# Down projection's held tiles prepared among earlier columns, mLSTM output transposes behind a step's gate products, forget gates a row chunk on, in a hybrid decoder layer

## The chip, the cores and the metric

One core of a Trainium2 chip runs the whole layer in one launch. The metric is the device time of one execution in microseconds; a kernel's time is the median of its runs. Matrix products run on TensorE (PE in the profile; its weight loads are PEld), elementwise work on VectorE (DVE) and ScalarE (ACT), and all loads are issued by SyncE's queue (SPq). Sums of products are kept in eight PSUM banks of 128 x 512 floats.

## The reference

One decoder layer on 256 tokens with a model width of 2048, all in float32:

```python
h = layer_norm(x) * (1.0 + sc1) + sh1
y = token_mixer(h, ...)                  # one input projection for everything below
x = layer_norm(ALPHA * x + g1 * y, ln_g[l, 0], ln_b[l, 0])
h = layer_norm(x) * (1.0 + sc2) + sh2
y = conv_ffn(h, w_up, conv_w, conv_b, w_down)
x = layer_norm(ALPHA * x + g2 * y, ln_g[l, 1], ln_b[l, 1])
...
# token_mixer: attention with gates (y_nsa) and mLSTM (y_ml), merged by gates
merged = sigmoid(merge_nsa) * (y_nsa @ w_br_nsa) + sigmoid(merge_ml) * (y_ml @ w_br_ml)
y = merged @ w_o
...
# mlstm, at its end: h normalised per head, times norm_g, times sigmoid(o)
# conv_ffn: (silu(causal_dwconv(a)) * g) @ w_down, with a and g of 5632 columns each
```

The shifts, scales and gates (sh, sc, g) come from a second input vector through a 2048 x 12288 product.

## The kernel before

Every weight is streamed once from memory in tiles of 512 KB. To keep float32 accuracy on TensorE, each weight tile w is split into a rounded part wh (ScalarE's cast, L154) and a remainder wl (VectorE's subtraction, L160), and each product is three matmuls: wh with the high and with the low part of the activations, and wl with the high part. `load_split` (L148 on) does load, cast and subtraction for one tile. There are seven w buffers, four wh and four wl (`WB`, L42). A load waits until a w buffer is free, a cast until a wh buffer is free, which is when TensorE has used the tile four places earlier.

The order of instructions on an engine is fixed when the program is built, and each engine takes its own in order: an instruction that waits holds up everything behind it on that engine. In places (`tc.manual_schedule`) the order is the order of the code for the engines named there; elsewhere a scheduler orders the instructions by what it reckons to be ready. Beside the main line, VectorE works off the conditioning product by multiply-accumulates on weight tiles (L279), spread over the whole kernel.

**Input projection.** Its last group of row chunks works through columns c = 0 to 5 with k the row chunk (loop at `for c in range(6)`, near L860). `steps` is a generator of the small gate computations of the mLSTM; `next(steps)` inside that loop (L873) moves it on by one step in the columns c = 3 and 4. Its product of the forget gates' cumulative sum is the PSUM tile ps_F, which waits for VectorE's subtraction at L706.

**Attention output and mLSTM output.** `nsa_out(g, t, ...)` gives the attention output of one group and one half of the rows in five steps for t = 1; in each step a block of probabilities is transposed on TensorE (ps_pT, L1044), ScalarE casts it (pT, L951), VectorE takes the remainder (vq or vx, L1055), and the products of earlier blocks are added into ps_y. `outs` (L1142) puts one tile of the merge gates' product (`fill(1)`, tile ps_mg, 12 matmuls) behind every step. In the last call, `outs(1, 1, ml_outs())`, the mLSTM output transposes `ml_out(h)` (L1119 on; four transposes into ps_yT, then y_mlT by ScalarE at L1128 and VectorE at L1129) are taken on by `next(beside, None)` ahead of the step's fill. ps_pT, ps_yT and ps_y share a pool of four PSUM banks, and ps_y keeps one. Branch products (ps_br with y_mlT and later with y_nsaT) are the next stage; the merge gates that are still in banks (ps_mg) must be emptied by two sigmoids (gt) before the branch product of y_nsaT can take their banks, and the gates kept in memory (gates0) are put through eight sigmoids (at L1203).

**Down projection, second half** (`proj_rows`, L1271 on, called with `hold`). The rows of the weight are 22 chunks of 128. The first 1536 output columns are three passes of 512 columns, each with 11 tiles (33 tiles), 12 matmuls a tile, for both halves of the rows (ps_d0, ps_d1). The last 512 columns are two half columns of 256, of six tiles each. The second of these uses held tiles: a tile is loaded, multiplied by the gate g2 on VectorE (L1306), cast on ScalarE into a kept buffer (L181) and given its remainder on VectorE (L182). They are held because the products of row half 1 come last, after all of row half 0. In the kernel before they are made inside the two half-column loops, and the scheduler spreads them over the end. After each pass VectorE adds the sum to the residual row (zt L1256, xz L1261) and takes statistics (L1265); the last residuals, the final layer norm and its stores follow (L1656 on).

Of the kernel before, what the change touches and what calls it, by code (L numbers as in the profile page):

```python
# [14 lines left out]
P = 128  # L15
# [15 lines left out]
NDOWN = 4 * 11  # L31
# [49 lines left out]
def build(ctx: ExitStack, tc: tile.TileContext, d, out, dbg=None):  # L81
    nc = tc.nc
# [44 lines left out]
    def load(src, after=None):  # L127
        n = src.shape[-1]
        t = wp.tile([P, 1024], F32, name="w", tag="w", bufs=WB[0])
        ins = nc.sync.dma_start(t[:, :n], src)  # L130
        if after:
            behind(ins, after)
        loaded[:] = [ins]
        return t
# [45 lines left out]
    def split_into(t, hi, lo):  # L180
        nc.scalar.copy(hi, t)  # L181
        nc.vector.tensor_sub(lo, t, hi)  # L182
# [260 lines left out]
    ready = [FIRST]  # L443
# [349 lines left out]
    for gi, kn in enumerate(GROUPS):  # L793
# [66 lines left out]
        for c in range(6):  # L860
            pss = [bank(psm, "ps_a%d" % t) for t in range(2)]
            aw = AW if c < 4 else 512
            for k in range(k0, k0 + kn):
                need(k)
                wh, wl = next(wa if c < 4 else wv)
                if k or c:
                    for t in range(2):
                        mm_a(pss[t][:, :aw], hT, k, t, wh, wl, k == k0, k == k0 + kn - 1)
                else:
                    for x, w in ((0, wh), (1, wh), (0, wl)):  # L870
                        for t in range(2):
                            mm(pss[t][:, :aw], hT[:, k, x, t * P:(t + 1) * P], turns(w), not x and w is wh, False)
                if not nxt and c in (3, 4) and (k - k0) % 3 == 2:  # L873
                    next(steps)
            for t in range(2):
                src = pss[t][:, :aw]
                if c < 4:
                    dst = projA[:, t, c * AW:(c + 1) * AW]
                else:
                    dst = mv1[:, t, 2 * c - 8:2 * c - 6, :MDV]  # L880
                    src = src.rearrange("p (h v) -> p h v", v=MDV)
                if gi == 0:
                    moved.append(lambda dst=dst, src=src: nc.scalar.copy(dst, src))
                else:
                    nc.vector.tensor_add(dst, src, dst)
            if not nxt:
                if c == 2:
                    while comp:
                        work()
                    Pk = pa.tile([P, 16, 48], F32R, name="Pk", tag="c4")  # L890
                    nTr = pa.tile([36, 384], F32R, name="nTr", tag="xe")
                    steps = gate_steps(Pk, nTr)
                    next(steps)
# [43 lines left out]
    def fill(n, rate=RATES[0]):  # L937

        for _ in range(n):
            if next(filler, 1) is None:  # L940
                tk.tick(rate)
# [177 lines left out]
    def ml_out(h):  # L1119
        ps = bank(psa, "ps_yT")  # L1120
        for c in range(2):
            for t in range(2):
                nc.tensor.transpose(ps[:, (2 * c + t) * P:(2 * c + t + 1) * P],
                                    num[:, h, t, c * P:(c + 1) * P], ident)
        for c in range(2):
            ng = prm[:, R_NG + 2 * h + c:R_NG + 2 * h + c + 1]
            src, hi = ps[:, c * S:(c + 1) * S], y_mlT[:, 2 * h + c, 0, :]
            nc.scalar.activation(hi, src, AF.Copy, scale=ng)  # L1128
            nc.vector.scalar_tensor_tensor(y_mlT[:, 2 * h + c, 1, :], src, ng, hi,  # L1129
                                           op0=ALU.mult, op1=ALU.subtract)  # L1130

    def ml_outs():
        for h in range(MH):
            yield
            ml_out(h)

    Ws, Pts = [], {}

    def probs(g, t):
        Pts[g, t] = nsa_probs(g, t)  # L1140

    def outs(g, t, beside=iter(())):  # L1142
        for _ in nsa_out(g, t, Pts.pop((g, t))):
            next(beside, None)
            fill(1)

    with tc.manual_schedule(engines={mybir.EngineType.PE}):
        fill(2, GR2)
        for _ in steps:
            pass  # L1150
        fill(2, GR2)
        for h in range(MH):
            Ws.append(ml_weights(h))
            fill(1)
        probs(0, 0)
        fill(2)
        num = pa.tile([P, MH, 2, MDV], F32, name="num", tag="m8")
        for h in range(MH):
            ml_num(h, Ws[h])
            if h % 2:  # L1160
                fill(h // 2 + 1)
        split_values()
        probs(0, 1)
        fill(3)
        outs(0, 0)
        probs(1, 0)
        fill(2)
        outs(0, 1)
        fill(1)
        probs(1, 1)  # L1170
        fill(2)
        norm = ml_norm()
        outs(1, 0, norm)
        run_all(norm)
        fill(3)
        y_mlT = p0.tile([P, 8, 2, S], F32R, name="y_mlT", tag="t16")
        outs(1, 1, ml_outs())
        fill(8 * (NU0 + NU1))
    dump("y_nsaT", y_nsaT.bitcast(F32))
    dump("y_mlT", y_mlT.bitcast(F32))  # L1180
# [87 lines left out]
        for _ in residual_steps(*args):  # L1268
            pass

    def proj_rows(xT, kn, w, base, grow, first, st, hold, rate, nm, hooks=()):  # L1271


        n = 0
        hooks = dict(hooks)
        for c in range(3 if hold else 4):
            pss = [bank(psm, "ps_%s%d" % (nm, t)) for t in range(2)]
            for i in range(kn // 2):
                wh, wl = load_split(w[base + n])
                n += 1  # L1280
                for j in range(2):
                    k = 2 * i + j
                    for t in range(2):
                        mm_a(pss[t], xT, k, t, wh[:, j * 512:(j + 1) * 512],
                             wl[:, j * 512:(j + 1) * 512], k == 0, k == kn - 1)
                tk.tick(rate)
                if n in hooks:
                    hooks[n]()
            for t in range(2):
                residual(pss[t], t, c * 512, 512, grow, first, st)  # L1290
        if not hold:
            return None
        later, fins = [], []
        for c in range(2):
            c0 = 1536 + 256 * c
            pss = [bank(psm, "ps_%s%d" % (nm, t)) for t in range(2)]
            for k0 in range(0, kn, 4):
                m = min(4, kn - k0)
                keep = hold(c, k0, m)
                if keep:  # L1300
                    t_ = load(w[base + n])
                    wh, wl = keep
                    v = t_[:, :m * 256].rearrange("p (k n) -> p k n", k=m)
                    if not first:
                        vv = v.rearrange("p k (a b) -> p k a b", a=2)
                        nc.vector.tensor_mul(vv, vv, grow[:, c0:c0 + 256].rearrange(  # L1306
                            "p (o b a) -> p o a b", o=1, a=2).to_broadcast([P, m, 2, P]))
                    if isinstance(wh, Chunks):
                        for j in range(m):
                            split_into(v[:, j], wh[:, j], wl[:, j])  # L1310
                    else:
                        split_into(v, wh, wl)
                else:
                    wh, wl = load_split(w[base + n], OFFA)
                    wh, wl = (x[:, :m * 256].rearrange("p (k n) -> p k n", k=m) for x in (wh, wl))
                n += 1
                tk.tick(rate)
                for t in range(2):
                    part = [lambda t=t, j=j, ps=pss[t], k=k0 + j, wh=wh, wl=wl:
                            mm_a(ps[:, :256], xT, k, t, wh[:, j], wl[:, j], k == 0, k == kn - 1)  # L1320
                            for j in range(m)]
                    if keep and t == 1:
                        later += part
                    else:
                        for f in part:
                            f()
            gate = None if keep and not first else grow
            fin = residual_steps(pss[1], 1, c0, 256, gate, first, st)
            residual(pss[0], 0, c0, 256, gate, first, st)
            marks["res%d" % c] = stats[-1]  # L1330
            if keep:
                fins.append(fin)
            else:
                run_all(fin)
        for f in later:
            f()
        return fins
# [309 lines left out]
    def hold(c, k, m):  # L1647
        if c == 0:
            return None
        h = hold3[:, k:k + m] if k < KD else hold2[:, k - KD:k - KD + m]  # L1650
        return h[:, :, 0], h[:, :, 1]

    fin, = proj_rows(uTt, KH, d["w_down"], NDOWN, g2, False, st3, hold, 0, "d")
    lg, lb = lnr2[:, 0, :], lnr2[:, 1, :]

    def store(t, c0, c1):  # L1656
# [176 lines left out]
```

## Time and profile before

| | |
|---|---|
| median of 3 runs | 1368.54 us (1368.25 to 1369.23) |
| profiled execution, its own time | 1369.19 us |
| span of its instructions | 1367.2 us |
| TensorE busy | 1346.4 us |
| VectorE busy | 1096.2 us |
| ScalarE busy | 733.4 us |
| memory traffic | 376.19 MB, mean 275 GB/s |

Time in the profile is counted from the first instruction. A row of the timeline gives start, duration, engine, line, operation, what is written and read, and in brackets how long the engine was idle before it and what released it. A matmul's duration includes its way through the array, so consecutive ones overlap; what counts is the distance of their starts, 0.216 us for 512 columns. A row of the chain of waits is start, duration, and what the end had to wait for. A row of waits gives total, number and longest.

### The profile page before, as it was taken

How to read it: one execution, taken by the hardware profiler on the slowest of the kernel's cores; microseconds unless marked ns; L12 is line 12 of the kernel's file. 1: busy time of each engine (PE TensorE's matmuls, PEld its weight loads, DVE VectorE, ACT ScalarE, POOL GpSimd, SP SyncE). 2: the span in 40 equal slices, each digit the busy share in tenths (PEclk: the TensorE clock that was granted, in tenths of full speed). 3: DMA queues.
4: the chain of work that ended last, by engine and by line, in shares of the span. 5: the costliest groups of instructions: out<-in, count | busy, mean ns of one | idle time of the engine just before them, and what ended most of it. 6: DMA issues, size and time to landing. Idle time of an engine off the chain costs nothing.

```text
span 1367.2 us, 20960 instructions
## 1 busy us (share of the span) xinstructions
PE 1346.4 (98%) x7874; PEld 1205.6 (88%) x7874; DVE 1096.2 (80%) x1657; ACT 733.4 (54%) x1052; POOL 3.6 (0%) x11
## 2 busy tenths in 40 slices
PE   7999999999999999999999999999999999999998
PEld 6999998888888888889799999988889999998887
DVE  8899978889898997878999888856556767666568
ACT  7654455646576444445765555544445555555442
POOL 0000000000000000000000000000000000000000
PEclk9999999999999999999999999999999999999999
DMA  9999988897877999996489888866666666666662
GB/s 383 418 419 386 382 325 298 322 320 249 308 270 273 384 342 322 398 350 221 144 311 307 294 279 303 283 216 200 202 204 202 202 201 202 202 202 201 201 201 78
DMA packets 104181, 376.19 MB, mean 275 GB/s; under 512 B 11248, under 2 KB 11792, under 8 KB 103568
## 3 DMA queue, kind: packets, MB, share of 16 engines
q1 hardware_dynamic: 104080, 374.86, 78.4%
q8 instruction: 61, 1.00, 0.3%
q14 instruction: 40, 0.33, 0.1%
HBM read 372.70 MB, written 2.11 MB: 274 GB/s over the span
## 4 chain that ended last, share of the span: by engine, by line
PE 80%; DVE 9%; DMA 6%; ACT 3%; issue 2%; SPq 0%; DVEq 0%; ACTq 0%
PE ps_up L112 32%; PE ps_d L112 14%; PE ps_mg L112 11%; PE ps_br L112 6%; PE ps_b L112 5%; PE ps_a L112 3%; PE ps_o L112 3%; DVE wl L160 2%; DMA w<-in_w_in_b_dram 2%; PE ps_u L112 2%; DMA w<-in_w_in_a_dram 1%; PE ps_s L112 1%; ACT wh L154 1%; DVE adaB L261 1%; DVE adaA L261 1%
## 5 line engine op out<-in xcount | busy, mean ns | idle before, releaser
L154 ACT CAST wh<-w 128x1024 fp32r<-128x1024 f32 (+1 forms) x470 | 484.8, 1036 | 498.7 <-PE ps_up L112 145.2
L160 DVE TENSOR_TENSOR wl<-w,wh 128x1024 fp32r<-128x1024 f32 (+1 forms) x468 | 561.2, 1205 | 227.5 <-ACT wh L154 224.3
L112 PE MATMUL ps_up<-h2T,wh 128*128 128x512 f32 x1344 | 440.6, 382 | 0.0
L112 PE MATMUL ps_up<-h2T,wl 128*128 128x256 f32 x1344 | 366.3, 273 | 0.0
L112 PEld LDWEIGHTS ps_up<-h2T,wh 128*128 128x128 f32 x1344 | 253.9, 189 | 35.4
L112 PEld LDWEIGHTS ps_up<-h2T,wl 128*128 128x128 f32 x1344 | 258.0, 192 | 0.1
L112 PE MATMUL ps_d<-wh,uTt 128*128 128x512 f32 (+1 forms) x704 | 198.5, 366 | 0.0
L279 DVE SCALAR_TENSOR_TENSOR w<-w,crow 128x1024 f32<-128x1024 f32 x132 | 160.7, 1219 | 0.0
L112 PE MATMUL ps_mg<-wh,hT 128*128 128x512 f32 x512 | 159.5, 383 | 0.0
L112 PEld LDWEIGHTS ps_d<-wh,uTt 128*128 128x128 f32 x704 | 129.9, 189 | 16.6
L112 PE MATMUL ps_d<-wl,uTt 128*128 128x512 f32 (+1 forms) x352 | 128.8, 366 | 1.0 <-DVE wl L160 1.0
L112 PE MATMUL ps_b<-hT,wh 128*128 128x256 f32 x768 | 124.4, 276 | 3.8 <-ACT hT L440 2.8
L112 PEld LDWEIGHTS ps_b<-hT,wh 128*128 128x128 f32 x768 | 110.9, 192 | 5.7 <-ACT hT L440 3.5
L112 PEld LDWEIGHTS ps_mg<-wh,hT 128*128 128x128 f32 x512 | 96.8, 189 | 14.2 <-issue 0.9
L112 PE MATMUL ps_a<-wh,hT 128*128 128x392 f32 (+1 forms) x384 | 102.8, 347 | 0.2 <-ACT wh L154 0.2
L112 PE MATMUL ps_mg<-wl,hT 128*128 128x512 f32 x256 | 97.2, 380 | 0.0
L112 PE MATMUL ps_b<-hT,wl 128*128 128x256 f32 x384 | 90.7, 275 | 0.0
L112 PEld LDWEIGHTS ps_d<-wl,uTt 128*128 128x128 f32 x352 | 66.7, 189 | 9.4 <-DVE wl L160 1.1
L112 PEld LDWEIGHTS ps_a<-wh,hT 128*128 128x128 f32 x384 | 69.2, 189 | 4.5 <-issue 1.0
L112 PE MATMUL ps_a<-wl,hT 128*128 128x392 f32 (+1 forms) x192 | 66.8, 349 | 1.3 <-DVE wl L160 1.2
L112 PEld LDWEIGHTS ps_b<-hT,wl 128*128 128x128 f32 x384 | 67.5, 192 | 0.1
L112 PE MATMUL ps_o<-wh,mgT 128*128 128x512 f32 x192 | 57.4, 379 | 0.0
(342 smaller groups left out, 1419.2 us busy)
## 6 DMA issues: line engine op xcount, KB each, us to landing
w<-in_w_up_dram SPq DMA_DIRECT2D x176, 512.0 KB, 4.4
w<-in_w_ada_dram SPq DMA_DIRECT2D x132, 512.0 KB, 5.1
w<-in_w_down_dram SPq DMA_DIRECT2D x89, 512.0 KB, 4.3
w<-in_w_mg_dram SPq DMA_DIRECT2D x64, 512.0 KB, 4.8
w<-in_w_in_b_dram SPq DMA_DIRECT2D x48, 512.0 KB, 11.0
w<-in_w_br_dram SPq DMA_DIRECT2D x32, 512.0 KB, 5.4
w<-in_w_o_dram SPq DMA_DIRECT2D x32, 512.0 KB, 5.4
adaA<-in_w_ada_dram SPq DMA_DIRECT2D x15, 1024.0 KB, 10.3
```

The costliest lines, as they stand in the source:

```text
L112: ins = nc.tensor.matmul(o, lhsT, rhs, start=start, stop=stop)
L154: hi = nc.scalar.copy(wh[:, :n], t[:, :n])
L160: lows.append(nc.vector.tensor_sub(wl[:, :n], t[:, :n], wh[:, :n]))
L261: ins = nc.vector.scalar_tensor_tensor(t, t, 1.0, crow, op0=ALU.mult, op1=ALU.mult, accum_out=parts[:, row(m), k, 0:1])
L279: ins = nc.vector.scalar_tensor_tensor(t, t, 1.0, crow[:, i * 1024:(i + 1) * 1024], op0=ALU.mult, op1=ALU.mult, accum_out=parts[:, row(m), ...
```

## The change

Three edits. In the down projection, the six held tiles of the second half column are made ahead: one of them behind each of the full tiles 13, 16, 19, 22, 25 and 28 of the 33. The code that makes one has become `keep_tile`, and the half-column loop takes the ready tile. In the mLSTM output, `ml_out(h)` stands ahead of the `yield`, and the generator is taken on behind a step's fill instead of ahead of it. In the input projection, the steps of the gate computations are given by a list of places: (3, 6) instead of (3, 5), the others as before.

```diff
-                if not nxt and c in (3, 4) and (k - k0) % 3 == 2:
+                if not nxt and (c, k - k0) in ((3, 2), (3, 6), (4, 2), (4, 5)):
                     next(steps)
...
     def ml_outs():
         for h in range(MH):
+            ml_out(h)
             yield
-            ml_out(h)
...
-    def outs(g, t, beside=iter(())):
+    def outs(g, t, beside=iter(()), behind_fill=iter(())):
         for _ in nsa_out(g, t, Pts.pop((g, t))):
             next(beside, None)
             fill(1)
+            next(behind_fill, None)
...
-        outs(1, 1, ml_outs())
+        outs(1, 1, behind_fill=ml_outs())
...
+        def keep_tile(c, k0, i):
...
+            t_ = load(w[i])
+            wh, wl = keep
+            v = t_[:, :m * 256].rearrange("p (k n) -> p k n", k=m)
+            if not first:
+                vv = v.rearrange("p k (a b) -> p k a b", a=2)
+                nc.vector.tensor_mul(vv, vv, grow[:, c0:c0 + 256].rearrange(
+                    "p (o b a) -> p o a b", o=1, a=2).to_broadcast([P, m, 2, P]))
...
+                split_into(v, wh, wl)
+            return wh, wl
...
                 if n in hooks:
                     hooks[n]()
+                if n in ahead:
+                    k0 = 4 * ahead.index(n)
+                    ready[k0] = keep_tile(1, k0, base + 3 * (kn // 2) + -(-kn // 4) + k0 // 4)
...
-                keep = hold(c, k0, m)
+                keep = ready[k0] if c and k0 in ready else keep_tile(c, k0, base + n)
...
-    fin, = proj_rows(uTt, KH, d["w_down"], NDOWN, g2, False, st3, hold, 0, "d")
+    fin, = proj_rows(uTt, KH, d["w_down"], NDOWN, g2, False, st3, hold, 0, "d", (), (13, 16, 19, 22, 25, 28))
```

VectorE in the down projection's first two passes. `wl` is a tile's remainder, `zt` and `xz` the residual after a pass, BN_STATS its statistics. Before, from the tiles of the first pass on:

```order
L160 TENSOR_TENSOR wl<-w,wh 128x1024 x8
L1256 TENSOR_TENSOR zt<-ps_d_12230,g_6795 128x512
L1256 TENSOR_TENSOR zt<-ps_d_12231,g_6795 128x512
L1261 TENSOR_TENSOR xz<-xz,zt 128x512 x2
L160 TENSOR_TENSOR wl<-w,wh 128x1024
L1265 BN_STATS st_0_12227<-xz 128x6 x2
L1265 BN_STATS st_1_12228<-xz 128x6 x2
```

And after, from the seventh and eighth tile on:

```order
L160 TENSOR_TENSOR wl<-w,wh 128x1024 x2
L1290 TENSOR_TENSOR w<-w,g_6795 128x1024
L160 TENSOR_TENSOR wl<-w,wh 128x1024
L182 TENSOR_TENSOR hold_12229<-w,hold_12229 128x4x256
L160 TENSOR_TENSOR wl<-w,wh 128x1024 x2
L1290 TENSOR_TENSOR w<-w,g_6795 128x1024
L160 TENSOR_TENSOR wl<-w,wh 128x1024
L182 TENSOR_TENSOR hold_12229<-w,hold_12229 128x4x256
L160 TENSOR_TENSOR wl<-w,wh 128x1024 x2
L1257 TENSOR_TENSOR zt<-ps_d_12230,g_6795 128x512
L1257 TENSOR_TENSOR zt<-ps_d_12231,g_6795 128x512
L1290 TENSOR_TENSOR w<-w,g_6795 128x1024
```

The held multiply (L1290, then still L1306) comes two wl behind the wl of the tile whose w buffer its load takes, or one: the load of the first is released by wl7 and its multiply stands behind wl8; those of the second to sixth are released by wl10, wl13, wl16, and the remainders (L182) of the fourth and fifth held tile. In SyncE's queue each of these loads stands behind the load of tile 13, 16, 19, 22, 25 and 28. Behind the third multiply stand two xz, wl15, two statistics, the third remainder, two statistics and wl16; the fourth multiply stands behind wl18, the fifth behind wl21, the sixth behind wl24, and between its remainder and wl26 stand two zt and one xz. On TensorE, in tiles 15 to 17, a wh product of row half 1 stands ahead of the first wl product, so that two wh products of tile 15 can run before its wl.

TensorE in the last five steps of the attention output; ps_mg are gate products, ps_br branch products, ps_pT and ps_yT the two kinds of transposes (the second of the four steps, as a difference):

```order
 L112 MATMUL ps_mg_4187<-wl,hT 128x512
 L112 MATMUL ps_mg_4187<-wh,hT 128x512
+L1123 MATMUL ps_yT<-head,num 128x128 x4
+L112 MATMUL ps_br_4461<-wh,y_mlT 128x512
+L112 MATMUL ps_br_4462<-wh,y_mlT 128x512
 L1044 MATMUL ps_pT<-head,pt 128x128 x4
 L112 MATMUL ps_y<-vq 128x512
 L112 MATMUL ps_y<-pT,vq 128x512 x2
-L112 MATMUL ps_br_4461<-wh,y_mlT 128x512
-L112 MATMUL ps_br_4462<-wh,y_mlT 128x512
-L1123 MATMUL ps_yT<-head,num 128x128 x4
```

The transposes of one head and two branch products have moved ahead of the step's pT. By the program's semaphores, ps_yT here waits for the vq of the first pT, and the pT behind it for the vq of the second pT; on VectorE that vq has a y_mlT (L1129) ahead of it now, which it had behind it.

ScalarE behind the cast of the last pT (the one with 48 rows), first before:

```order
L951 CAST pT<-ps_pT 48x512
L1203 ACT_TABLE_LOAD
L1203 ACTIVATE gates_3079<-gates_3079 128x512 x8
L1128 ACTIVATE y_mlT<-ps_yT,prm 128x256
L154 CAST wh<-w 128x1024
L1064 CAST y_nsaT<-ps_y 128x4x128
L1203 ACTIVATE gt<-ps_mg_4186 128x512
L1203 ACTIVATE gt<-ps_mg_4187 128x512
```

and after:

```order
L951 CAST pT<-ps_pT 48x512
L1204 ACT_TABLE_LOAD
L1204 ACTIVATE gates_3079<-gates_3079 128x512 x8
L154 CAST wh<-w 128x1024 x2
L1064 CAST y_nsaT<-ps_y 128x4x128
L1204 ACTIVATE gt<-ps_mg_4186 128x512
L1204 ACTIVATE gt<-ps_mg_4187 128x512
```

The y_mlT of the last head has moved ahead of that cast and a wh cast has come behind the sigmoids. On TensorE 32 branch products of y_mlT stand ahead of that last pT now and 20 before. The first branch product of y_nsaT waits for the first gt.

At ps_F nothing has moved: it stands at the same row on TensorE with the same waits, and the orders of all engines are the same up to the stage of the mLSTM output.

More of the change, by code (lines that the diff above doesn't have):

```diff
@@ L1269, in residual, with proj_rows @@
             pass
-    def proj_rows(xT, kn, w, base, grow, first, st, hold, rate, nm, hooks=()):
+    def proj_rows(xT, kn, w, base, grow, first, st, hold, rate, nm, hooks=(), ahead=()):
         n = 0
         hooks = dict(hooks)
+        ready = {}
+        def keep_tile(c, k0, i):
+            c0, m = 1536 + 256 * c, min(4, kn - k0)
+            keep = hold(c, k0, m)
+            if not keep:
+                return None
+            t_ = load(w[i])
[5 more added lines that the diff above has]
+                    "p (o b a) -> p o a b", o=1, a=2).to_broadcast([P, m, 2, P]))
+            if isinstance(wh, Chunks):
+                for j in range(m):
+                    split_into(v[:, j], wh[:, j], wl[:, j])
+            else:
+                split_into(v, wh, wl)
+            return wh, wl
         for c in range(3 if hold else 4):
@@ L1298, in proj_rows @@
                 m = min(4, kn - k0)
-                keep = hold(c, k0, m)
+                keep = ready[k0] if c and k0 in ready else keep_tile(c, k0, base + n)
                 if keep:
-                    t_ = load(w[base + n])
                     wh, wl = keep
[L1303 to L1312, printed above, removed]
                 else:
```

## The prediction

> **What bounds the kernel now.** I read the page first, for who is busy and what the last chain consists of.
>
> ```profile
> span 1367.2 us, 20960 instructions
> PE 1346.4 (98%) x7874; PEld 1205.6 (88%) x7874; DVE 1096.2 (80%) x1657; ACT 733.4 (54%) x1052; POOL 3.6 (0%) x11
> PE 80%; DVE 9%; DMA 6%; ACT 3%; issue 2%; SPq 0%; DVEq 0%; ACTq 0%
> w<-in_w_down_dram SPq DMA_DIRECT2D x89, 512.0 KB, 4.3
> ```
>
> TensorE is busy for 98% of the span, so an edit can only give back a part of the 20.8 us in which it stands still, and anything that makes it stand still longer is paid in full unless a later standstill absorbs it. So I asked next for busy time by stage, cut at the places that the change touches. The columns are the stretch, its length and each engine's busy time in it.
>
> ```profile
> 405.33:444.29 38.96, 38.28 (x191) 32.55 (x189) 32.55 (x48) 23.89 (x36) 0.00 (x0) 1.00 0.80 271
> 444.29:620.00 175.71, 175.71 (x832) 153.89 (x831) 152.24 (x202) 79.72 (x87) 0.53 (x1) 1.00 0.94 350
> 620.00:1241.00 621.00, 620.24 (x3605) 558.76 (x3604) 467.85 (x758) 347.46 (x501) 0.00 (x0) 1.00 0.72 233
> 1241.00:1326.50 85.50, 85.50 (x399) 74.87 (x398) 50.78 (x57) 37.15 (x38) 0.00 (x0) 1.00 0.64 197
> 1326.50:1350.00 23.50, 22.55 (x201) 22.36 (x200) 22.36 (x31) 8.98 (x9) 0.00 (x0) 1.00 0.29 91
> ```
>
> The stretch with the mLSTM output transposes (405 to 444) has a little slack; from 444 to 1326 TensorE stands still for 0.76 us in all, so a delay made at 405 to 444 arrives at the end whole. The 33 full tiles of the down projection (1241 to 1326.5) have no gap at all: 85.5 / 33 = 2.59 us a tile. The two half columns lose 0.95 us. The change therefore has little to win: about 1 us in the half columns, about 1 us in the transposes' stretch.
>
> **Down projection, the gain.** In the timeline of the end, TensorE's one gap, its last held product, and the two residuals of VectorE are:
>
> ```profile
> 1336.98 0.38 PE L112 MATMUL ps_d<-wl,uTt 128*128 128x256 f32 x1 [0.95 <-DVE wl L160]
> ...
> 1357.18 1.88 PE L112 MATMUL ps_z<-xz,head 128*128 128x512 f32 x4
> ```
> ```profile
> 1350.65 0.41 DVE L1261 TENSOR_TENSOR xz<-xz,ps_d 128x256 f32<-128x256 f32 x1
> ...
> 1357.59 0.41 DVE L1261 TENSOR_TENSOR xz<-xz,ps_d 128x256 f32<-128x256 f32 x1
> ```
>
> The wl of a half tile came late because six held tiles (multiply, cast, low part) sat among them on VectorE. With these gone the 0.95 goes. What is late next: after the change the last half column runs 66 products for row half 0 and then 66 for row half 1, so the first sum is ready 66 x 0.11 = 7.3 us before the second, and VectorE's work from the first residual to the second is 1357.59 - 1350.65 = 6.94 us. TensorE stays last, by 0.4 us. Gain 1.05 us (0.7 to 1.2).
>
> **Down projection, the cost.** The same six tiles now stand among tiles 9 to 26 on VectorE. The rows that price it:
>
> ```profile
> 1250.07 1.22 DVE L160 TENSOR_TENSOR wl<-w,wh 128x1024 fp32r<-128x1024 f32 x1 [0.93 <-ACT wh L154]
> 1252.66 1.23 DVE L160 TENSOR_TENSOR wl<-w,wh 128x1024 fp32r<-128x1024 f32 x1 [1.37 <-ACT wh L154]
> ...
> 1269.34 1.28 DVE L1256 TENSOR_TENSOR zt<-ps_d,g 128x512 f32<-128x512 f32 x2
> 1270.54 1.29 DVE L1261 TENSOR_TENSOR xz<-xz,zt 128x512 f32<-128x512 f32 x2
> 1271.74 1.22 DVE L160 TENSOR_TENSOR wl<-w,wh 128x1024 fp32r<-128x1024 f32 x1
> 1272.88 1.40 DVE L1265 BATCH_NORM_STATS2 st<-xz 128x6 f32<-128x256 f32 x4
> ...
> 1322.91 1.55 DVE L1306 TENSOR_TENSOR w<-w,g 128x1024 f32<-128x1024 f32 x1 [1.69 <-DMA w<-in_w_down_dram]
> ...
> 1325.57 1.23 DVE L182 TENSOR_TENSOR hold<-w,hold 128x1024 fp32r<-128x1024 f32 x1
> ```
>
> In steady state wl7 runs at 1250.07 and wl8 at 1252.66; tile k's first wl product is due at 1241.2 + 2.59 (k - 1), so a wl is 5.3 us early. That is the cover. What eats it: the multiply of a held tile waits for a load issued only one or two wl earlier, and VectorE takes its queue in order, so the next tile's wl waits too. The row at 1322.91 shows that very wait (1.69 us) in the kernel before, where it has one wl ahead of it. How long a load takes is in the chain of waits:
>
> ```profile
> 1318.66 4.15 DMA w<-in_w_down_dram
> ...
> 1325.62 5.16 DMA w<-in_w_down_dram
> ```
>
> A load alone takes 4.15 us; the one at 1325.62, with another issued 1.2 us after it, 5.16. In the new order the second and third held loads follow other loads closely, so I take 5.0 for these two and 4.6 for the rest. A held tile costs VectorE 1.3 (multiply) and 1.2 (low part) beside its wait. Step by step (H1 to H6 are the held tiles, in VectorE's new order):
>
> H1: issued at 1251.3 when wl7 ends, in by 1255.6; multiply to 1257.0, wl9 1258.2, low part 1259.4, wl10 1260.6. H2: issued at 1260.6, in by 1265.6, while VectorE has only wl11 (to 1261.8); multiply to 1266.9, wl12 1268.1, low part 1269.3, wl13 1270.5. H3: issued then, in by 1275.5; before it wl14 and two zt (1.3); multiply to 1276.8, two xz to 1278.0, wl15 to 1279.2. Tile 15's wl is due at 1277.9 (two wh products of tile 15 now run ahead of it): TensorE waits 1.3. Before wl16 stand four statistics (1.4) and the low part (1.2), so wl16 ends 3.8 after wl15 where a tile lasts 2.6: 1.2 more. H4, issued at 1283.0, in by 1287.6: wl19 at 1290.1, due 1290.8. H5, issued at 1291.3: wl22 at 1298.4, just in time. H6, issued at 1299.6, in by 1304.2: multiply (half size, 0.7), wl25, low part, two zt, one xz, wl26 at 1309.8, due 1308.9: 0.9. Sum 3.4 us.
>
> The same sum with 4.3 (the page's median) for every load gives 1.2 (only wl16), with 5.2 for every load 6.4 (2.5, 1.2, 1.1, 0.5, 1.1). I take 3.4, between them, because the close spacing holds for some loads and not for others; 1.2 and 6.4 stay for the range. Net of the gain: +2.35 (0 to +5.7). ScalarE's casts of these tiles cost nothing: it is busy 37 of 85.5 us here.
>
> By the Trainium skill (DMA: Bandwidth & Descriptors, Anatomy of one DMA) a transfer takes some 2.0 us plus its bytes at 436 GB/s; for 512 KB I estimate 3.2 us from that, with which no wl would be late and the sum would be that of rival 1 below. The trace disagrees: 4.15 at the least here.
>
> **mLSTM output transposes.** TensorE, then ScalarE, then VectorE, in the stretch where four steps of the attention output alternate with gate products:
>
> ```profile
> 409.23 0.60 PE L1044 MATMUL ps_pT<-head,pt 128*128 128x128 f32 x4
> ...
> 409.89 0.59 PE L112 MATMUL ps_y<-pT,vq 128*128 128x512 f32 x2
> 410.54 0.70 PE L112 MATMUL ps_br<-wh,y_mlT 128*128 128x512 f32 x2
> 411.86 0.66 PE L1123 MATMUL ps_yT<-head,num 128*128 128x128 f32 x4 [0.62 <-DVE vq L1055]
> ...
> 422.95 0.60 PE L1044 MATMUL ps_pT<-head,Pk 128*48 128x128 f32 x4
> ...
> 432.63 0.38 PE L112 MATMUL ps_br<-wh,y_nsaT 128*128 128x512 f32 x1
> ```
> ```profile
> 409.43 1.05 ACT L154 CAST wh<-w 128x1024 fp32r<-128x1024 f32 x1 [1.95 <-PE ps_mg L112]
> ...
> 423.58 0.58 ACT L951 CAST pT<-ps_pT 48x512 fp32r<-48x512 f32 x1 [0.55 <-PE ps_pT L1044]
> 424.18 1.28 ACT L1203 ACT_TABLE_LOAD   x1
> 425.47 4.27 ACT L1203 ACTIVATE gates<-gates 128x512 f32<-128x512 f32 x8
> 429.65 0.46 ACT L1128 ACTIVATE y_mlT<-ps_yT,prm 128x256 fp32r<-128x256 f32 x1
> 430.01 1.03 ACT L154 CAST wh<-w 128x1024 fp32r<-128x1024 f32 x1
> ...
> 431.42 1.08 ACT L1203 ACTIVATE gt<-ps_mg 128x512 f32<-128x512 f32 x2
> ```
> ```profile
> 409.98 1.22 DVE L279 SCALAR_TENSOR_TENSOR w<-w,crow 128x1024 f32<-128x1024 f32 x1
> ...
> 411.12 0.68 DVE L1055 TENSOR_TENSOR vq<-ps_pT,pT 128x512 fp32r<-128x512 f32 x1
> 411.72 0.47 DVE L1129 SCALAR_TENSOR_TENSOR y_mlT<-ps_yT,prm,y_mlT 128x256 fp32r<-128x256 f32 x1
> ```
>
> TensorE was through with the two branch products at 410.97 (two steps of 0.216 after 410.54) and waited until 411.86, 0.89, for vq, which gives back the bank that the transposes write; 0.22 more went between 410.32, when the pieces before were issued, and 410.54, on the wh cast that ends at 410.48. Now the gate products run to 409.2, the transposes to 409.6, and then come the two branch products and the next pT. First, the branch products still need that cast (it starts when TensorE frees the buffer, at 409.4, as before), and only 0.36 us of transposes stand ahead of them where pT and its three products (409.23 to 410.32, 1.1) stood: a wait of 0.9 instead of 0.22. Second, the next pT, at 410.9, needs the same vq, which now has one y_mlT (0.4 until its successor starts) ahead of it and ends at 412.2: with the release 1.37 instead of 0.89. So 2.27 for 1.11, +1.2.
>
> Third, further on. Ahead of the fourth pT (422.95) stand 12 more branch products (2.6) and one more block of transposes (0.36); with the 1.2 just lost TensorE comes to it at 427.1. Behind its cast ScalarE has, in order, the table load and eight sigmoids of the gates, two wh casts, the cast of y_nsaT and the two sigmoids that empty the gate banks. From the rows, 423.58 to 431.42 was 7.84 us; less the y_mlT (0.36 until its successor starts) and with one more wh cast (0.93) it is 8.4. The cast now starts at 427.7, so the first gt sigmoid starts at 436.1 and ends at 436.7. The first y_nsaT branch product needs its bank. TensorE gets there at 434.8: a wait of 1.9 where there was none at 432.63. Less 0.2 us for fewer switches and small gaps, the edit costs +2.9 (2.0 to 3.6). Nothing behind it waits until the end (the stage rows above), so it is all paid.
>
> **Forget gates.** The steps that come earlier leave the forget gates' product at the same place among TensorE's instructions, with the same waits, and every engine's order the same until 405 us. So this part does not do what it says, and costs and brings 0; the wait that it is about stays:
>
> ```profile
> PE ps_F L112 <- DVE sm L706: 0.7, 1, 0.7
> ```
>
> **Sum.** The profiled run took 1369.19 us, 1.99 more than its span and 0.65 above the median of 1368.54. +2.35 + 2.9 + 0 = +5.25: 1374.4 for that run, 1373.8 for the median. Bounds: 0 + 2.0 = +2.0 to 5.7 + 3.6 = +9.3, with loads all slow; +8.5 is as far as I take it.
>
> **Rivals.** (1) The held loads are in time, on the other side of the line. If they land in less than about 3.8 us (the step above with 3.8 leaves wl16 0.2 late and no other), the columns cost nothing and the gain of 1.05 remains; with the transposes' +2.9 that is +1.85, 1370.4, not slower by what can be measured (0.2%, 2.7 us, is about what a measurement of this kernel tells from no change). Against it: 4.15 is the least of the rows above. (2) The transposes give what was lost: vq is done before its pT and ScalarE's sigmoids are through in time; the 1.1 of waits goes and none comes. With +2.35 that is +1.2, 1369.8. Against it: ScalarE's chain of 8.4 us starts from the fourth pT, which the order puts 4 us later. (3) Both: -2.2, 1366.4; and with the forget gates' 0.7 as well, 1365.7. (4) All held loads take 5.2 us: +5.35 + 2.9 = +8.25, 1376.8.
>
> **How the numbers follow.** Forecast 0.66, rival 1 0.13, rival 2 0.09, rival 3 0.04, rival 4 0.08. The range takes the forecast, rival 4 and rival 1, with most of rival 2: 1369.0 to 1377.0. Faster by over 0.2%: only rival 3 and what I do not see, 0.05. Within: rivals 1 and 2, 0.22. Slower: 0.73.
>
> **What would show it.** Right: in the columns waits of TensorE's ps_d for wl, at tiles 15 and 16 above all, with VectorE's held multiply waiting for its DMA by 3 us or more ahead of them; no gap in the half columns; near 435 us a wait of ps_br for ScalarE's gt, and a wait of pT for vq near 411. Wrong: a gapless 1241 to 1326.5 (rival 1), or gate products that start again at or before 444.3 (rival 2).

## The result, and the profile after

| | before | after |
|---|---|---|
| median | 1368.83 us (6 runs, 1368.25 to 1369.31) | 1376.46 us (6 runs, 1374.26 to 1377.85) |
| profiled execution | 1369.19 us | 1376.34 us |
| its span | 1367.2 us | 1374.5 us |

The change makes the kernel slower by 0.55%: the ratio is 1.0055 with a 95% interval of 1.0042 to 1.0068. That is 7.6 us by the medians and 7.3 by the spans; 5.25 was forecast, with 1377.0 as the upper end of the range.

The first lines of the page of after: the same work, 4.4 us more in which TensorE counts as busy and 2.9 more in which it stands still.

```profile
span 1374.5 us, 20960 instructions
PE 1350.8 (98%) x7874; PEld 1208.8 (88%) x7874; DVE 1096.7 (80%) x1657; ACT 731.6 (53%) x1052; POOL 3.6 (0%) x11
PE 79%; DVE 9%; DMA 5%; issue 3%; ACT 3%; SPq 0%; DVEq 0%; ACTq 0%
```

The waits of TensorE in after, longest first in total (total, times, longest), without those of the first 100 us:

```profile
PE ps_d L112 <- DVE wl L160: 3.2, 2, 2.7
...
PE ps_br L112 <- ACT gt L1204: 1.6, 1, 1.6
...
PE ps_pT L1044 <- DVE vq L1055: 1.0, 1, 1.0
...
PE ps_br L112 <- ACT wh L154: 0.7, 1, 0.7
```

All four are in places that the prediction named. In TensorE's timeline:

```profile
411.05 0.70 PE L112 MATMUL ps_br<-wh,y_mlT 128*128 128x512 f32 x2 [0.70 <-ACT wh L154]
412.77 0.66 PE L1044 MATMUL ps_pT<-head,pt 128*128 128x128 f32 x4 [1.02 <-DVE vq L1055]
...
437.23 0.48 PE L112 MATMUL ps_br<-wh,y_nsaT 128*128 128x512 f32 x1 [1.58 <-ACT gt L1204]
...
1283.85 0.48 PE L112 MATMUL ps_d<-wl,uTt 128*128 128x512 f32 x1 [2.66 <-DVE wl L160]
...
1314.56 0.48 PE L112 MATMUL ps_d<-wl,uTt 128*128 128x512 f32 x1 [0.49 <-DVE wl L160]
```

And VectorE's in the first two passes of the down projection, the held multiplies with their waits:

```profile
1258.79 1.54 DVE L1290 TENSOR_TENSOR w<-w,g 128x1024 f32<-128x1024 f32 x1 [1.59 <-DMA w<-in_w_down_dram]
...
1268.96 1.53 DVE L1290 TENSOR_TENSOR w<-w,g 128x1024 f32<-128x1024 f32 x1 [3.94 <-DMA w<-in_w_down_dram]
...
1279.99 1.46 DVE L1290 TENSOR_TENSOR w<-w,g 128x1024 f32<-128x1024 f32 x1 [3.69 <-DMA w<-in_w_down_dram]
1281.37 1.29 DVE L1262 TENSOR_TENSOR xz<-xz,zt 128x512 f32<-128x512 f32 x2
1282.57 1.22 DVE L160 TENSOR_TENSOR wl<-w,wh 128x1024 fp32r<-128x1024 f32 x1
```

The second and third wait together are 7.6 us in which no remainder is made, and the remainder of tile 15 follows at 1282.57. In the chain of waits of after, the loads behind these two rows:

```profile
1263.83 5.04 DMA w<-in_w_down_dram
...
1274.00 5.90 DMA w<-in_w_down_dram
```

Behind the wait at tile 15 comes something that the prediction did not have. Two stretches in a row (length, then TensorE's busy time; the granted clock is the third figure from the end):

```profile
1281.35:1284.76 3.41, 0.91 (x4) 0.83 (x5) 3.41 (x7) 3.27 (x4) 0.00 (x0) 1.00 0.00 0
1284.76:1288.17 3.41, 3.41 (x10) 2.71 (x9) 3.41 (x5) 1.12 (x2) 0.00 (x0) 0.50 0.79 208
```

From 1284.76 to 1288.17 us the granted clock was half and matmuls followed each other at 0.43 us instead of 0.216. That is busy time on the page, and 1.8 us lost.

How late a matmul of after starts against the one with the same number in before gives the account (the difference of the two traces' start times):

| place | late by, us | step |
|---|---|---|
| input projection, at 220 us | 1.1 | |
| behind the forget gates' product, at 264 us | 0.5 | -0.6 |
| ahead of the transposes, at 405 us | 0.5 | |
| gate products again, at 446 us | 3.4 | +2.9 |
| down projection's start | 3.3 | -0.1 |
| tile 15's first remainder product | 6.1 | +2.8 |
| behind the slow stretch | 7.9 | +1.8 |
| end of the full tiles | 8.7 | +0.8 |
| last half column | 7.5 | -1.2 |
| end | 7.3 | -0.2 |

The first 1.1 us are not the change's. They come from a stretch of half clock near the start, which the profile of before lacks:

```profile
25.24:28.65 3.41, 3.41 (x17) 3.41 (x18) 3.18 (x5) 2.67 (x5) 0.00 (x0) 0.50 1.03 416
```

A second profile of the changed kernel (the last experiment below) lacks it too, and four profiles of other kernels have one between 19 and 29 us.

### The profile page after: what moved, and what is told of

Read it like the earlier page. It is cut to its first block, busy times and chain, and to the rows that moved or that the text cites. A ratio compares the mean times of both kernels' runs of the same rounds, so it can differ in the third digit from the quotient of the medians.

```text
span 1374.5 us, 20960 instructions
## 1 busy us (share of the span) xinstructions
PE 1350.8 (98%) x7874; PEld 1208.8 (88%) x7874; DVE 1096.7 (80%) x1657; ACT 731.6 (53%) x1052; POOL 3.6 (0%) x11
## 4 chain that ended last, share of the span: by engine, by line
PE 79%; DVE 9%; DMA 5%; issue 3%; ACT 3%; SPq 0%; DVEq 0%; ACTq 0%
PE ps_up L112 32%; PE ps_d L112 13%; PE ps_mg L112 11%; PE ps_b L112 6%; PE ps_br L112 6%; DVE wl L160 4%; PE ps_a L112 3%; PE ps_o L112 3%; DMA w<-in_w_down_dram 2%; PE ps_u L112 2%; ACT wh L154 1%; DMA w<-in_w_in_b_dram 1%; PE ps_s L112 1%; DVE adaB L261 1%; DVE adaA L261 1%
```

## The experiments

Each ratio is against runs of the kernel before on the same chip, and microseconds beside a ratio are worked out from it and the median of those runs. "Alone" means that the other two edits are undone.

**Each edit alone.** The down projection's edit (`keep_tile` and the places 13, 16, 19, 22, 25, 28), nothing else:

> The kernel before with the down projection's edit alone. Theory (the held multiplies stand on VectorE one or two remainders behind loads that take 4.3 to 6 us, so TensorE runs out of remainders in the first columns): TensorE waits over 2 us at tile 15 and again near tile 26, no gap in the half columns, about +4 us in all (in the trace of after the columns cost 5.4 us and the half columns gave back 1.2). Rival (the columns' waits come from the 3.3 us by which this stage started later after the other edits): no waits in the columns and about -1.1 us.

Measured: 1.0036 (1.0025 to 1.0048), +4.9 us. The rival falls: the stage starts on time here and waits all the same. TensorE's waits:

```profile
PE ps_d L112 <- DVE wl L160: 5.2, 5, 2.7
```
```profile
1280.49 0.48 PE L112 MATMUL ps_d<-wl,uTt 128*128 128x512 f32 x1 [2.73 <-DVE wl L160]
1284.06 0.48 PE L112 MATMUL ps_d<-wl,uTt 128*128 128x512 f32 x1 [0.71 <-DVE wl L160]
1292.57 0.48 PE L112 MATMUL ps_d<-wl,uTt 128*128 128x512 f32 x1 [0.68 <-DVE wl L160]
1301.07 0.48 PE L112 MATMUL ps_d<-wl,uTt 128*128 128x512 f32 x1 [0.46 <-DVE wl L160]
1312.45 0.48 PE L112 MATMUL ps_d<-wl,uTt 128*128 128x512 f32 x1 [0.67 <-DVE wl L160]
```

The wait at tile 15 is that of after, without the slow stretch; the later waits, which the slow stretch had covered, are there. Counted by start times, the five cost 3.0, 1.0, 1.0, 0.7 and 0.9, in all 6.6 us, and the half columns give back 1.2. So the passes lose more here at full clock than in after with the slow stretch (5.4).

The mLSTM output transposes' edit:

```diff
         for h in range(MH):
+            ml_out(h)
             yield
-            ml_out(h)
...
-        outs(1, 1, ml_outs())
+        outs(1, 1, behind_fill=ml_outs())
```

> The kernel before with the mLSTM output transposes' edit alone. Theory: TensorE's waits at the branch products (0.7), at the next pT (1.0) and at the first branch product of the attention output (1.6) appear as in after; +2.9 us. Rival (they need the other edits' timing): the waits of before stay and the time is within 0.5 us of before.

Measured: 1.0023 (1.0014 to 1.0031), +3.1 us, with the three waits as in after:

```profile
PE ps_br L112 <- ACT gt L1204: 1.6, 1, 1.6
PE ps_pT L1044 <- DVE vq L1055: 1.0, 1, 1.0
PE ps_br L112 <- ACT wh L154: 0.7, 1, 0.7
```

The forget gates' edit, (3, 6) for (3, 5):

> The kernel before with the forget gates' edit alone. Theory (every engine's order is the same as before): the 0.7 us wait of ps_F for VectorE is there whenever the input projection is on time, and the time differs by under 0.5 us. Rival (the edit takes the wait away, as the trace of after seems to show): no wait at ps_F, -0.6 us.

Measured: 1.0003 (0.9988 to 1.0019). The order of instructions is that of before on every engine, so this is the kernel before under another name, and the wait is there in this run too:

```profile
PE ps_F L112 <- DVE sm L706: 0.5, 1, 0.5
```

In the trace of after the wait was gone because TensorE came to it 1.1 us late from the start of the kernel; the -0.6 in the account above is a wait that took up a delay, not a gain. In the second profile of the changed kernel, where TensorE is on time, the wait is there:

```profile
258.23 0.80 PE L112 MATMUL ps_F<-sm,prm 128*128 128x4 f32 x6 [0.58 <-DVE sm L706]
```

**What in the down projection costs: work, place or lead.** First the multiply later, its load and its amount as in the change:

```diff
-                nc.vector.tensor_mul(vv, vv, ...)
+                mul = nc.vector.tensor_mul(vv, vv, ...)
+                if ahead:
+                    behind(mul, lows[-1])
```

> The down projection's edit alone, with each held multiply ordered behind the remainder of the tile whose load it follows: loads as early as in the change, multiplies five or six tiles later, the work the same. Theory (the wait for the load, not the work, is what costs): no wait of TensorE in the columns or the half columns, VectorE's held multiplies wait for no load, -1.1 us. Rival (15 us of VectorE work and six more loads are too much for the columns wherever they stand): TensorE waits for remainders behind the first pass and the time is at or above before's.

Then the load earlier and the multiply where the change has it, or nearly: in the passes the load of a held tile stands behind tile n - 3 instead of n, and the multiply is ordered behind the remainder six back (`lows[-6]`).

> The down projection's edit alone, with each held load issued three tiles earlier than in the change and the multiplies at nearly the places they have in it. Theory (the cost is the short lead of the load over its multiply on an in-order VectorE, not where the work stands): the held multiplies wait for no load or under 1 us each, TensorE's waits near tile 15 and 16 go or fall under 1 us in all, and the time is -1.2 to +0.5 us against before. Rival (VectorE's work so early in the passes, beside the first pass's residual, is what costs): a wait of over 1.5 us near tile 15 stays, +2 us or more.

Measured: 0.9999 (0.9990 to 1.0008) and 0.9997 (0.9988 to 1.0005). In neither does TensorE wait in a pass or a half column, or a held multiply for its load; VectorE's only waits in this stage are the usual ones. Its line for the kernel with later multiplies, then for the one with earlier loads:

```profile
DVE wl L160 <- ACT wh L154: 23.7, 19, 1.4
```
```profile
DVE wl L160 <- ACT wh L154: 23.5, 22, 1.4
```

The second kernel has its first three held multiplies at the same places among the remainders as the change. So neither the 15 us of work nor its place costs anything; the short lead of the load does. The half columns give back 1.2 us in both profiles, but the medians differ from before's by -0.2 and -0.8 us only, with no change inside the intervals. The traces of the other kernels say why that gain is not firm: the gap of 0.95 us in the half columns, against which it is counted, is not always there. Five traces have the order of before in this stage on TensorE, VectorE and ScalarE. The gap is in two of them, before and the forget gates' edit alone:

```profile
1336.12 0.38 PE L112 MATMUL ps_d<-wl,uTt 128*128 128x256 f32 x1 [0.72 <-DVE wl L160]
```

In the three kernels with the transposes' edit and without this one, TensorE has no wait in the half columns. In these three, one held multiply waited for its load there or just ahead, and two did in the other two; what decides it was not tried.

Then only the third multiply later (`if ahead and k0 == 8: behind(mul, lows[-1])`):

> The down projection's edit alone, with only the third held multiply ordered behind the remainder of the tile whose load it follows. Theory (each held load's wait eats the cover by itself; the 2.7 us at tile 15 is the third wait on top of two and the first pass's residual): the waits at tiles 15 and 16 go, later ones of 0.5 to 0.7 may stay, the half columns gain 1.2: between -0.7 and +1.5 us. Rival (the third only takes the place of what the first pass's residual does to the cover anyway): a wait of over 1.5 us near tile 15 or 16 stays and the time is over +2.5.

Measured: 1.0024 (1.0014 to 1.0033), +3.3 us, and neither theory nor rival: the time is the rival's, the place of the wait is not. The waits near tiles 15 and 16 went, and a wait of 1.72 came instead further on:

```profile
1297.85 0.48 PE L112 MATMUL ps_d<-wl,uTt 128*128 128x512 f32 x1 [1.72 <-DVE wl L160]
...
1309.61 0.48 PE L112 MATMUL ps_d<-wl,uTt 128*128 128x512 f32 x1 [0.67 <-DVE wl L160]
```

The held tiles that still follow their loads closely eat the cover one after the other; taking one out moves the place where it runs out.

Then the held tiles closer together, two full tiles apart (13, 15, 17, 19, 21, 23):

> The down projection's edit alone, with the held tiles two full tiles apart instead of three (behind tiles 13, 15, 17, 19, 21, 23). Theory (a held tile costs VectorE 2.7 us of work and a wait for its load of 2 to 4 us with all behind it standing; two remainders more are 2.4, so a period of two tiles needs 7 to 9 us where TensorE takes 5.2): a wait of 2 to 3.5 us for nearly every held tile once the cover is gone, 10 to 15 us in all, and the granted clock falling below 1 in stretches behind the longer ones. Rival (the cost is the work's sum, the same 15 us as in the change): about the change's +4 to +5.

Measured: 1.0006 (0.9997 to 1.0015). Both were wrong by far: the same work in a shorter stretch costs less, with one wait of TensorE in place of five. VectorE's waits for held loads, and TensorE's one wait in the passes:

```profile
DVE w L1289 <- DMA w<-in_w_down_dram: 5.8, 3, 2.7
```
```profile
1281.69 0.48 PE L112 MATMUL ps_d<-wl,uTt 128*128 128x512 f32 x1 [0.77 <-DVE wl L160]
```

5.8 us of waits instead of 16.3 in after. My count of a period had taken the wait as a constant of a held tile. It goes with the lead, which one can count in the orders: the number of tiles by which the multiply stands ahead of the tile behind whose load its own load is issued. In the change that is 5, 5, 5, 4, 4, 4, with waits of 1.6 to 3.9 us. With the closer places it is 5, 4, 4, 4, 3, 3: waits of 1.7, 2.7 and 1.4, and none for the rest. With the loads three tiles earlier it is about 2, with the later multiplies none or less, and there is no wait. The lead is not all of it: at 4 the waits are 2.2 to 2.5 us in the change, and 2.7, 1.4 and none with the closer places.

**The transposes.** With ScalarE's sigmoids of the kept gates ordered behind those that empty the gate banks:

```diff
             if dst[t] is src[t]:
                 behind(ins, marks["last"])
+                behind(ins, marks["gt"])
+            else:
+                marks["gt"] = ins
```

> The mLSTM output transposes' edit alone, with ScalarE's eight sigmoids of the kept gates ordered behind the two that empty the gate banks. Theory (the third wait of that edit, 1.6 us at the first branch product of the attention output, is the queue on ScalarE behind the last pT's cast: table load and 4.3 us of sigmoids that nobody needs yet): that wait goes, the two near 411 us (0.7 and 1.0) stay, and of +2.9 us about +1.2 is left. Rival (TensorE waits there for something else too, the gate multiplies or a remainder, and finds the next wait): +2.5 or more.

And with the first head's y_mlT on VectorE ordered behind the second vq as well:

> The same with VectorE's remainder of the first head's y_mlT ordered behind the second vq, which the second pT waits for. Theory (that vq has moved behind a y_mlT of 0.4 us on VectorE): the wait of pT for vq falls from 1.0 to 0.6 us, the wait of the branch products for the wh cast (0.7) stays, about +0.8 us against before. Rival (vq is set by the cast ahead of it, not by VectorE's queue): 1.0 stays, +1.2.

Measured: 1.0009 (1.0000 to 1.0018) and 1.0003 (0.9995 to 1.0012), +1.2 and +0.4 us. TensorE's waits in this stretch, first with the sigmoids moved, then with both:

```profile
PE ps_pT L1044 <- DVE vq L1055: 1.0, 1, 1.0
PE ps_br L112 <- ACT wh L154: 0.7, 1, 0.7
PE ps_br L112 <- ACT gt L1204: 0.4, 1, 0.4
```
```profile
PE ps_br L112 <- ACT wh L154: 0.7, 1, 0.7
PE ps_pT L1044 <- DVE vq L1055: 0.6, 1, 0.6
PE ps_br L112 <- ACT gt L1208: 0.4, 1, 0.4
```

The wait for gt falls from 1.6 to 0.4, and that for vq from 1.0 to 0.6 when a y_mlT no longer stands ahead of it: two queues, on ScalarE and VectorE, make 1.6 of the edit's 2.9 us. (By start times the stretch costs 1.7 us with the sigmoids moved and 1.3 with both.) What remains is no better than before, since the branch products wait for a wh cast that TensorE itself releases.

**A version that beats both.** The later multiplies, and ps_F ordered on TensorE behind the last product of the third row chunk of column 4, which is what the third edit's name says and its list of places did not do:

```diff
+                    if marks_F and (c, k - k0) == (4, 2):
+                        behind(marks_F.pop(), chunk_last)
                     next(steps)
```

> The down projection's edit with the later multiplies, and the forget gates' product (ps_F) made to stand seven products (1.5 us) later on TensorE by an order of its own, which is what the change's third edit did not do. Theory: the half columns give back 1.2 us and the wait at ps_F (0.7 to 0.9) goes: 1.2 to 2.1 us under before. Rival (the steps that hang on ps_F come late in turn): a new wait of TensorE at one of the steps behind it (the transposes ps_uT, ps_mc, ps_sc) and no more than -1.2.

Measured: 0.9989 (0.9980 to 0.9998), -1.5 us against before, with the interval's end just under no change, and some 9 under the change. The product stands seven products (1.5 us) later on TensorE than before, and waits for nothing:

```profile
259.36 0.73 PE L112 MATMUL ps_F<-sm,prm 128*128 128x4 f32 x6
```

**The slow stretch.** With the wait at tile 15 made longer, by two more passes of VectorE over the third held tile (times zero plus itself, so its values stay) and the statistics ahead of the remainder:

> The down projection's edit alone with two more passes of VectorE over the third held tile (multiplying by zero and adding: the values stay) and the first pass's statistics ahead of tile 15's remainder: TensorE's wait there grows from 2.7 to about 6.5 us. Theory (the granted clock falls when TensorE has stood still through a window of some 3 us, so 2.7 us does it at times and 6.5 always): matmul steps of 0.43 instead of 0.22 us for some 3 us behind that wait, 1.5 to 1.8 us more. Rival (the slow stretch in the trace of after has nothing to do with the wait): full clock behind it.

and the changed kernel a second time:

> The changed kernel as it is, a second look. Theory (the slow stretch behind the wait at tile 15 depends on when the wait falls): either the wait of 2.6 to 2.8 us with slow steps behind it and fewer waits later, or the wait without slow steps and waits of 0.5 to 1 us at later held tiles; 1374 to 1378 us either way.

Each was run once, at 1375.81 and 1376.62 us. The waits, with TensorE's busy time and the clock around them, first with the longer wait, then in the changed kernel:

```profile
1284.02 0.79 PE L112 MATMUL ps_d<-wl,uTt 128*128 128x512 f32 x1 [5.72 <-DVE wl L160]
```
```profile
1280.23:1283.64 3.41, 0.00 (x0) 0.00 (x0) 3.41 (x7) 0.78 (x1) 0.00 (x0) 1.00 0.00 0
1283.64:1287.06 3.42, 3.04 (x7) 2.50 (x8) 3.42 (x4) 1.21 (x2) 0.00 (x0) 0.50 0.55 158
```
```profile
1283.90 0.80 PE L112 MATMUL ps_d<-wl,uTt 128*128 128x512 f32 x1 [2.60 <-DVE wl L160]
```
```profile
1280.16:1283.57 3.41, 1.14 (x6) 0.66 (x4) 3.41 (x4) 2.03 (x3) 0.00 (x0) 1.00 0.02 10
1283.57:1286.99 3.42, 3.09 (x7) 2.52 (x8) 3.42 (x7) 1.86 (x2) 0.00 (x0) 0.50 0.52 164
```

The wait grew to 5.7, not 6.5, and the slow steps cost 1.6 us in both. So far: half clock behind waits of 2.60, 2.66 and 5.72, full clock behind 2.73 (the edit alone) and behind 1.72. So the length of the wait alone does not decide. What fits is where the wait lies. Each stretch of half clock lasted 3.41 us, and in after the two of them, at 25.24 and 1284.76 us, start 369 times 3.413 us apart, as if time were cut into slots of that length. The slot ahead of the slow one had TensorE idle for 2.50 us of 3.41 in after, 2.27 in the second profile of the change, and all of it with the longer wait. In the edit alone the slots can be counted on from its half clock at 19.05 to 22.46 us; there an edge cuts the wait of 2.73 into 0.80 and 1.93, and the clock stays full:

```profile
1275.15:1278.56 3.41, 2.61 (x13) 1.94 (x11) 1.89 (x2) 0.43 (x1) 0.00 (x0) 1.00 0.21 83
1278.56:1281.98 3.42, 1.49 (x7) 1.33 (x8) 3.42 (x6) 3.42 (x4) 0.00 (x0) 1.00 0.21 31
1281.98:1285.39 3.41, 2.69 (x13) 2.05 (x12) 3.41 (x6) 1.08 (x2) 0.00 (x0) 1.00 0.85 237
```

This reading came after the runs, and none was made to test it. It holds for these five waits in the passes, where 2.27 us of a slot or more brought half clock and 1.94 or less (the slot ahead of the two shown with the longer wait) did not. At the start of the kernel, with other products, idle time alone does not sort the slots: 1.69 us of one were followed by half clock in after, and 1.80 by full clock in before.

## Why the prediction was right, and what it mis-sized

The direction, the places of the waits and what each waits for were right, and the time was inside the range, half a microsecond under its end: nearer to rival 4 (1376.8) than to the forecast (1374.4 for the profiled run). That it stayed inside is in part luck, since 1.8 us of it are a term that the prediction did not have.

**Transposes, +2.9 forecast, +2.9 measured.** The three waits were put at 0.9, 1.37 and 1.9 us, of which 0.22 and 0.89 had been there; the trace has 0.70, 1.02 and 1.58 as idle time, and 2.9 in all by start times (2.9 in the second profile too). The steps that give them, the y_mlT ahead of vq and the sigmoids ahead of gt, are shown by the two experiments that took them away. Rival 2 falls.

**Half columns, -1.05 forecast, -1.2 measured** (in every trace with this edit, with another 0.2 at the very end). No gap is left there. But the prediction took the gap of one profile for a property of the kernel, and three traces with the same order lack it; against those the edit gains 0.2 to 0.4 us.

**Forget gates, 0 forecast, 0 measured**, by the kernel with this edit alone and the same order of instructions.

**Columns, +3.4 forecast, +5.4 measured.** This is the step that was mis-sized, at the third held load. I took 5.0 us for it; the six held loads of after took 4.06, 5.04, 5.90, 4.32, 4.59 and 4.60. (The sum also has 4.3 for the first, where its text says 4.6.) Behind a held multiply the next instruction came 1.38 to 1.48 us after its start and not 1.3. With this, tile 15's first remainder product came 2.8 late and not 1.3; up to the third load the forecast's times, moved by the 3.3 us, are the trace's within 0.2. The wait of 1.2 at tile 16 is missing and 1.8 us of half clock stand in its place: slow matmuls give VectorE time. The last wait (0.8) was forecast (0.9). So the waits make 3.6 us against 3.4, but only because too little at tile 15 and too much at tile 16 cancel.

The edit alone, without half clock, shows the size of the miss: +4.9 us for the down projection by the runs and 5.2 by the traces (6.6 less 1.2 and 0.2), where +2.35 was forecast. The forecast's own sum with 5.2 us for every load (rival 4: 2.5, 1.2, 1.1, 0.5, 1.1, in all 6.4) is close to it step by step (3.0, 1.0, 1.0, 0.7, 0.9, in all 6.6), though its loads were not all slow: 4.20, 5.07, 5.84, 5.71, 4.48 and 4.57. With the third and fourth slow, the later held tiles run out of cover as well. A reason for slow loads was in the rows of before, and I gave it too little weight, but it is argued and not shown: once VectorE has stood and then makes remainders back to back, w buffers come free together and the next loads go out 1.1 to 1.2 us apart. The row of before at 1325.62 with a second load 1.2 us behind took 5.16; in the edit alone three loads issued 1.1 us apart from 1284.04 on landed after 5.7, 5.9 and 6.0. Against it, three issued as closely in after from 1287.40 on took 4.3, 4.7 and 4.8, and in the second profile of the change the third held load took 5.30, with nearly the same wait at tile 15.

The prediction's "4.15 at the least" was the least of the rows of the chain, not of the loads. For the loads of this weight from 1244 to 1345 us the profile of before has:

```profile
DMA to landing us min/median/max: 3.4/4.3/5.2
```

Rival 1 needed under 3.8 us and falls here, since no held load in after landed under 4.06. The Trainium skill (DMA: Bandwidth & Descriptors, Anatomy of one DMA) gives the sum behind the 3.2 us for transfers issued by GpSimd. The loads here are issued by SyncE, so that estimate was for another path, and no load of that row was so fast.

**The clock was no term at all.** The prediction counted a wait of TensorE as its own length. The Trainium skill (TensorE: Matmul & The Clock Gate, What's actually happening) says that the clock falls to half after an idle window of some 3.4 us, and that the window runs free of the kernel. The half clock (0.50), the length of 3.41 us and the fixed slots of the rows above agree, but here a slot in which TensorE stood for 2.27 or 2.50 us was enough.

## What to carry to other kernels

Moving a load and the work on it ahead together hides nothing: on an engine that takes its queue in order, count how many instructions stand between what frees the load's buffer and the first use of the load, and give that the longest time that such loads take in the traces (up to 6 us here, where the median in before was 4.3), not the median. Once an engine is late, its buffers come free one after the other and the next loads crowd, so the slow case is the one to size by. A delay on TensorE is paid whole unless a later wait takes it up. A wait of about 2.6 us or more may in addition bring a stretch of half clock (1.6 to 1.8 us here), which can in turn cover later waits. And a gap seen in one profile is worth a second profile before it is counted as a gain.

## What the runs showed of the hardware that was not expected

- The 512 KB loads of the down projection took 3.4 to 5.2 us in before. In the edit alone three issued 1.1 us apart took 5.7 to 6.0, and in after three issued as closely took 4.3 to 4.8.
- Behind waits of TensorE of 2.60, 2.66 and 5.72 us the granted clock was 0.5 for a stretch of 3.41 us, with 0.43 us from one 512-column matmul to the next. One of 2.73 us left it at full speed. In after two such stretches start a whole number of times 3.413 us apart.
- The same held multiply took 1.34 us in the last stage of before and 1.53 in the columns, where a load and remainders ran beside it. Which of these slows it was not tried.
- The changed kernel's six runs spread over 3.6 us and the six of before beside them over 1.1. Such a spread is not the change's alone: of 29 runs of before beside the later multiplies, single ones reached 1374.48 us, 6 above their median.
